# Second layer norm of an encoder block: scale and offset shared by VectorE, ScalarE and GpSimd, with gain and bias in PSUM

## The chip, the cores and the metric

The kernel runs on one core of one Trainium2 chip. The metric is device time in microseconds for one execution of the whole program; the median of three runs of the kernel before is 1250.47 us (1249.44 to 1252.44). Engines are named as in the profile: PE is TensorE, DVE is VectorE, ACT is ScalarE, POOL is GpSimd, and SP is SyncE, which issues most transfers. A name with a q (SPq, POOLq) is that engine's sequencer.

## The reference

One block of a bidirectional encoder over 1024 tokens of width 1024: a token mixer (projection, pooling, banded attention, gates), a layer norm, a mixture of 32 experts with two experts per token, and a second layer norm. The change is in the last line only.

```python
def layer_norm(x, g, b):
    xf = x.astype(jnp.float32)
    mu = jnp.mean(xf, axis=-1, keepdims=True)
    var = jnp.mean(jnp.square(xf - mu), axis=-1, keepdims=True)
    return ((xf - mu) * lax.rsqrt(var + LN_EPS) * g.astype(jnp.float32)
            + b.astype(jnp.float32)).astype(x.dtype)
...
        x = layer_norm(ALPHA * x + mix, ln1_g[l], ln1_b[l])
        ffn = hier_moe(x, w_router_group[l], b_router_group[l], w_router_expert[l],
                       b_router_expert[l], w_gate[l], w_up[l], w_down[l])
        x = layer_norm(ALPHA * x + ffn, ln2_g[l], ln2_b[l])
```

Here everything is float32, and `ln2_g`, `ln2_b` are vectors of 1024 numbers that lie along the free dimension of a tile, so they can't be given to an engine as one number per partition; mean and reciprocal root can.

## The kernel before

Tokens are cut into NT = 8 tiles of 128, one token per partition. Up to about 1209 us the program runs the mixer, the first layer norm and the expert blocks, with TensorE nearly always busy. The expert blocks add their outputs into the buffer `accd` in device memory, which already holds ALPHA times the first norm's result. A loop of zero or more rounds follows for tokens over an expert's capacity (`tc.For_i`, L1469; none here), with a barrier of all engines behind it. Then comes the second layer norm, the only part that the change touches, from L1491 to L1561.

In it SP loads the eight tiles `R[0]` to `R[7]` of 512 KB from `accd` (L1497); in the trace their tile is `r`. `MV[i0]` (`mv` in the trace) holds six columns for each tile of a pair: 0 the mean, 1 the variance, 2 the reciprocal root, 3 the square root, 4 a scaled mean of ACT's statistics, 5 minus half of the variance plus epsilon. `ln_gb2` (`ln_gb` in the trace) holds gain `ln_g2` and bias `ln_b2`, each copied to all partitions, in SBUF.

Statistics of a tile come from DVE (`stats_dve`, two BATCH_NORM_STATS2 and one AGGREGATE; tiles 0 and 2) or from ACT (`stats_act`, two passes with accumulation; tiles 1 and 3 to 7). `root` on ACT takes the square root, and `rstd2` on DVE makes the reciprocal root with one Newton step, for two tiles at a time: RECIPROCAL, two TENSOR_TENSOR, one SCALAR_TENSOR_TENSOR, each on 128x2 numbers. Then DVE alone passes twice over each tile: `scale` (L1536), (R - mean) * gain, and `finish2` (L1540), R * rstd + bias, behind which SP stores the tile (L1541). The last tile's second pass and store are cut in halves.

The order on each engine is the order in which the code is written (`tc.manual_schedule()`); each engine works its own list in order and waits by semaphores. Stores stand in SP's queue in the order written, too, and each waits there for its tile.

POOL has nothing to do in this part. Earlier it runs two-input elementwise work: L869 and L870 of the first layer norm (gain and bias, 128x1024), and L746, the low part of a split. The lines L826 and L827 (`rstd_of`) are DVE's own small steps there, on 128x1 numbers: both read two operands from SBUF. L92 is the helper `split`; where it reads `pT`, one operand lies in PSUM and the other in SBUF. L849 adds a PSUM tile to an SBUF tile.

Of the kernel before, what the change touches and what calls it, by code (L numbers as in the profile page):

```python
# [11 lines left out]
F32 = mybir.dt.float32  # L12
# [3 lines left out]
AF = mybir.ActivationFunctionType  # L16
ALU = mybir.AluOpType
AX = mybir.AxisListType
PSUM = bass.MemoryType.PSUM
# [3 lines left out]
D = 1024  # L23
NT = S // 128
# [9 lines left out]
EPS = 1e-5  # L34
# [15 lines left out]
def kernel(  # L50
# [8 lines left out]
    out = out[0]  # L59
# [7 lines left out]
    act, dve, pe, pool, sp = nc.scalar, nc.vector, nc.tensor, nc.gpsimd, nc.sync  # L67
# [6 lines left out]
    def bigtile(shape, dt, name):  # L74
        return big.tile(shape, dt, name=name, tag="b")
# [24 lines left out]
    HALF = [slice(0, 512), slice(512, 1024)]  # L100
# [383 lines left out]
    for b in range(NT + FILLS):  # L484
# [7 lines left out]
        if b >= NT:  # L492
            name = ("gate", "gate2")[b - NT]
# [904 lines left out]
    SPLIT, room, q = [], [], 0  # L1398
    for t, (b, p, c) in enumerate(SEQ):
        q = max(q, LOADS.index((p, c)))  # L1400
# [60 lines left out]
    ln_gb2 = bigtile([128, 2, D], F32, "ln_gb2")  # L1461
    ln_g2, ln_b2 = ln_gb2[:, 0], ln_gb2[:, 1]
    sp.dma_start(ln_g2, bcast(ln2_g, D))
    sp.dma_start(ln_b2, bcast(ln2_b, D))
    epst = const.tile([128, 1], F32, name="epst")
# [26 lines left out]
    R = {}  # L1492
    for i in range(0, NT, 2):
        t = bigtile([128, 2, D], F32, "r2")
# [2 lines left out]
            sp.dma_start(R[i + q], accd[(i + q) * 128:(i + q + 1) * 128])  # L1497


    MV = {}  # L1500
    for i0 in range(0, NT, 2):
        MV[i0] = lp2.tile([128, 2, 6], F32, name="mv2", bufs=NT // 2)

    def col(i, c):
        return MV[i - i % 2][:, i % 2, c:c + 1]

    def stats_act(i):

        junk = lp2.tile([128, D], F32, name="junk", bufs=1)
        act.activation(junk, R[i], AF.Copy, scale=-1.0 / (32 * D), accum_out=col(i, 4))  # L1510
        act.activation(col(i, 0), col(i, 4), AF.Copy, scale=-32.0)
        act.activation(junk, R[i], AF.Square, scale=1.0 / 32, bias=col(i, 4), accum_out=col(i, 1))  # L1512

    def stats_dve(i):
        st = lp2.tile([128, 2, 6], F32, name="bnst2")
        for c in range(2):
            dve.bn_stats(st[:, c, :], R[i][:, HALF[c]])
        dve.bn_aggr(MV[i - i % 2][:, i % 2, 0:2], st)

    def root(i0):  # L1520

        mv = MV[i0]
        act.activation(mv[:, :, 3], mv[:, :, 1], AF.Sqrt, bias=epst)  # L1523
        act.activation(mv[:, :, 5], mv[:, :, 1], AF.Copy, scale=-0.5, bias=-0.5 * EPS)

    def rstd2(i0):

        mv = MV[i0]
        r, t, u = mv[:, :, 2], mv[:, :, 3], mv[:, :, 5]
        dve.reciprocal(r, t)  # L1530
        dve.tensor_mul(t, r, r)  # L1531
        dve.tensor_mul(t, t, u)  # L1532
        dve.scalar_tensor_tensor(r, t, 1.5, r, op0=ALU.add, op1=ALU.mult)  # L1533

    def scale(i):
        dve.scalar_tensor_tensor(R[i], R[i], col(i, 0), ln_g2, op0=ALU.subtract, op1=ALU.mult)  # L1536

    def finish2(i):
        for sl in HALF if i == NT - 1 else [slice(0, D)]:
            dve.scalar_tensor_tensor(R[i][:, sl], R[i][:, sl], col(i, 2), ln_b2[:, sl], op0=ALU.mult, op1=ALU.add)  # L1540
            sp.dma_start(out[i * 128:(i + 1) * 128, sl], R[i][:, sl])  # L1541

    act.activation(lp2.tile([128, 1], F32, name="rt"), epst, AF.Sqrt)
    stats_dve(0)
    stats_act(1)
    root(0)
    stats_dve(2)
    stats_act(3)
    root(2)
    scale(0)  # L1550
    for i in range(4, NT):
        stats_act(i)
        if i % 2:
            root(i - 1)
    for i0 in range(0, NT, 2):
        if i0:
            scale(i0)
        scale(i0 + 1)
        rstd2(i0)
        finish2(i0)  # L1560
        finish2(i0 + 1)  # L1561


# [73 lines left out]
```

## Time and profile before

| | |
|---|---|
| median of 3 runs | 1250.47 us |
| the profiled execution's own time | 1252.02 us |
| its span in the profile | 1250.2 us |
| PE busy | 1157.9 us (93% of the span) |
| DVE busy | 907.7 us (73%) |
| ACT busy | 751.0 us (60%) |
| POOL busy | 264.8 us (21%) |
| the last expert block's matmuls end | about 1208.7 us |
| first load of the second layer norm is issued | 1214.75 us |
| last pass of DVE ends | 1246.0 us |

Times inside the profile are microseconds from the start of the span. The profiled execution took 1.8 us more than its span, and 1.55 us more than the median of the runs. The chain of waits is followed back from the last instruction; the timeline lists instructions in order of time with their duration, and "x2" stands for two of the same kind that follow each other; the windows view gives the busy time of each engine in a stretch. An instruction's duration in the timeline includes time that it spends waiting for something other than a semaphore.

### The profile page before, as it was taken

The page shows a single profiled execution, that of the slowest core. Times are in us where ns is not written, and L with a number is a line of the kernel's source. Part 1 is how long each engine was busy: PE and PEld are TensorE (multiplying, and loading weights), DVE is VectorE, ACT ScalarE, POOL GpSimd, SP SyncE. Part 2 cuts the span into 40 slices and gives each one's busy share as a digit, 9 for nine tenths or more (in the row PEclk, how much of TensorE's full clock was granted, in tenths as well). Part 3 has the DMA queues.
Part 4 walks back from the last instruction along what each step waited for, and adds up shares of the span by engine and source line. Part 5 has one row for each costly group of instructions (what it writes and reads, how often), then busy time and mean ns, then how long its engine had stood idle before and what let it go on. Part 6 is the DMA issues. An engine that isn't in the chain of part 4 may idle for free. (4 is left out here: it accounts for less than half of the span.)

```text
span 1250.2 us, 16049 instructions
## 1 busy us (share of the span) xinstructions
PE 1157.9 (93%) x5645; PEld 878.4 (70%) x5645; DVE 907.7 (73%) x1282; ACT 751.0 (60%) x989; POOL 264.8 (21%) x216
## 2 busy tenths in 40 slices
PE   8999999999999998999589999999999989989960
PEld 8888878888888886888468767766766656655630
DVE  4788972221853326899879999999978989988857
ACT  5577772111231114454458888888877887888745
POOL 2322200000000002466312222231222221232010
PEclk9999999999999998999689999999999999999995
DMA  8000104111121125635788999999999999999956
GB/s 272 1 1 1 45 17 122 51 51 42 35 76 40 37 102 183 263 135 217 240 320 327 366 390 396 364 375 374 351 330 357 348 391 376 365 385 395 400 159 236
DMA packets 91631, 279.36 MB, mean 223 GB/s; under 512 B 18989, under 2 KB 50733, under 8 KB 67869
## 3 DMA queue, kind: packets, MB, share of 16 engines
q1 hardware_dynamic: 83261, 252.15, 53.6%
q0 software_dynamic: 8288, 26.17, 8.4%
q8 instruction: 45, 0.74, 0.2%
q14 instruction: 37, 0.30, 0.1%
HBM read 252.32 MB, written 25.97 MB: 223 GB/s over the span
## 5 line engine op out<-in xcount | busy, mean ns | idle before, releaser
L1058 DVE TENSOR_TENSOR wel<-we,weh 128x2048 fp32r<-128x2048 f32 (+1 forms) x193 | 427.3, 2244 | 58.3 <-ACT weh L1056 56.6
L1056 ACT ACTIVATE weh<-we 128x2048 fp32r<-128x2048 f32 (+1 forms) x193 | 356.8, 1877 | 30.3 <-PE up L97 6.7
L1365 POOL DMA_INDIRECT accd<-y,psl x29 | 70.8, 2442 | 364.9 <-ACT y L1364 326.0
L646 ACT ACTIVATE sig<-gps,bch 128x512 f32<-128x512 f32 x29 | 19.9, 687 | 169.0 <-PE gps L98 169.0
L98 PE MATMUL gps<-xh,ghl 128*128 128x512 f32 x296 | 115.3, 390 | 0.0
L96 PE MATMUL gps<-xh,ghl 128*128 128x512 f32 x296 | 115.2, 389 | 0.0
L97 PE MATMUL gps<-xl,ghl 128*128 128x512 f32 x296 | 115.1, 389 | 0.0
L92 DVE TENSOR_TENSOR ghl<-wraw,ghl 128x1024 fp32r<-128x1024 f32 (+1 forms) x26 | 26.4, 1020 | 82.5 <-ACT ghl L91 82.5
L97 PE MATMUL gate<-wel,xinT 128*128 128x512 f32 (+7 forms) x176 | 70.8, 402 | 4.5 <-DVE wel L1058 4.5
L96 PE MATMUL yp<-weh,hT 128*128 128x512 f32 (+7 forms) x176 | 73.1, 415 | 0.1
L96 PE MATMUL gate<-weh,xinT 128*128 128x512 f32 (+7 forms) x176 | 70.7, 402 | 0.1
L98 PE MATMUL gate<-weh,xinT 128*128 128x512 f32 (+7 forms) x176 | 69.9, 397 | 0.0
L98 PE MATMUL yp<-weh,hT 128*128 128x512 f32 (+7 forms) x176 | 69.8, 397 | 0.0
L97 PE MATMUL yp<-wel,hT 128*128 128x512 f32 (+7 forms) x176 | 69.6, 395 | 0.0
L96 PE MATMUL up<-weh,xinT 128*128 128x512 f32 (+7 forms) x176 | 69.5, 395 | 0.0
L97 PE MATMUL up<-wel,xinT 128*128 128x512 f32 (+7 forms) x176 | 68.9, 391 | 0.0
L98 PE MATMUL up<-weh,xinT 128*128 128x512 f32 (+7 forms) x176 | 68.9, 391 | 0.0
L96 PEld LDWEIGHTS gps<-xh,ghl 128*128 128x128 f32 x296 | 55.6, 188 | 11.7
L97 PEld LDWEIGHTS gps<-xl,ghl 128*128 128x128 f32 x296 | 55.6, 188 | 11.6
L98 PEld LDWEIGHTS gps<-xh,ghl 128*128 128x128 f32 x296 | 55.6, 188 | 11.6
L1268 POOL DMA_INDIRECT xin<-x1d,psl x29 | 55.1, 1900 | 12.1 <-issue 5.2
L96 PE MATMUL z<-woh,mhl 128*128 128x512 f32 x128 | 52.7, 412 | 4.3 <-DVE sig L668 4.3
(342 smaller groups left out, 2690.4 us busy)
## 6 DMA issues: line engine op xcount, KB each, us to landing
we<-in_w_gate_dram SPq DMA_DIRECT2D x62, 1024.0 KB
we<-in_w_up_dram SPq DMA_DIRECT2D x62, 1024.0 KB
we<-in_w_down_dram SPq DMA_DIRECT2D x60, 1024.0 KB
wraw<-in_w_in_dram SPq DMA_DIRECT2D x20, 512.0 KB
x<-in_x_dram SPq DMA_DIRECT2D x8, 512.0 KB
wo<-in_w_o_dram SPq DMA_DIRECT2D x4, 1024.0 KB
xr<-in_x_dram SPq DMA_DIRECT2D x8, 512.0 KB
x1d<-x1p SPq DMA_DIRECT2D x8, 512.0 KB
```

The costliest lines, as they stand in the source:

```text
L92: dve.tensor_sub(lo, src, f(hi))
L96: pe.matmul(ps, lh, rh, start=first, stop=False)
L97: pe.matmul(ps, lh, rl, start=False, stop=False)
L98: pe.matmul(ps, ll, rh, start=False, stop=last)
L646: act.activation(dst[:, HALF[half]], ps, fn, bias=bch[:, bcol:bcol + 1])
L1056: act.activation(hi[:, sl], raw, AF.Copy)
L1058: dve.tensor_sub(lo[:, sl], raw, f(hi[:, sl]))
L1268: pool.indirect_dma_start(out=XIN[b][:n], out_offset=None, in_=x1d, in_offset=bass.IndirectOffsetOnAxis(ap=slot0 if b == 0 else IDX[b][:n, ...
L1365: pool.indirect_dma_start(out=accd, out_offset=bass.IndirectOffsetOnAxis(ap=IDX[b][:n, 0:1], axis=0), in_=y[:n], in_offset=None, compute_o ...
```

## The change

The gain and the bias are first copied by ACT into a PSUM tile `gbp` (four pieces of 128x512). The passes over the tiles are then divided:

- Tile 0: POOL alone, a TENSOR_SCALAR (subtract the mean, multiply by rstd) and two TENSOR_TENSOR (gain, bias).
- Tile 1: ACT does the normalisation (`Identity` with scale and bias; DVE makes the bias -mean * rstd, L1577), POOL gain and bias.
- Tiles 2, 3, 4: DVE does `scale` with the gain from PSUM in two halves, ACT multiplies by rstd (`times`), POOL adds the bias.
- Tiles 5, 6, 7: DVE does `scale` and `offset`, both in halves with the second operand from PSUM.

The statistics of tiles 4 and 6 go from ACT to DVE. `root` and `rstd2` run for tile 0 and tile 1 apart. SP's stores stand in the order 0, 1, 5, 2, 6, 3, 7 (two halves); tile 4 is stored from ACT's queue at its end.

```diff
--- before.py
+++ after.py
@@ -1497,6 +1497,13 @@
             sp.dma_start(R[i + q], accd[(i + q) * 128:(i + q + 1) * 128])
 
 
+    lpp = ctx.enter_context(tc.tile_pool(name="lpp", bufs=1, space=PSUM, reuse_waits="tile"))
+    gbp = lpp.tile([128, 2, D], F32, name="gbp")
+    for c in range(2):
+        for half in range(2):
+            act.activation(gbp[:, c, HALF[half]], ln_gb2[:, c, HALF[half]], AF.Copy)
+
+
     MV = {}
     for i0 in range(0, NT, 2):
         MV[i0] = lp2.tile([128, 2, 6], F32, name="mv2", bufs=NT // 2)
@@ -1517,48 +1524,88 @@
             dve.bn_stats(st[:, c, :], R[i][:, HALF[c]])
         dve.bn_aggr(MV[i - i % 2][:, i % 2, 0:2], st)
 
-    def root(i0):
-
-        mv = MV[i0]
-        act.activation(mv[:, :, 3], mv[:, :, 1], AF.Sqrt, bias=epst)
-        act.activation(mv[:, :, 5], mv[:, :, 1], AF.Copy, scale=-0.5, bias=-0.5 * EPS)
-
-    def rstd2(i0):
-
-        mv = MV[i0]
-        r, t, u = mv[:, :, 2], mv[:, :, 3], mv[:, :, 5]
+    def root(*ii):
+
+        mv, q = MV[ii[0] - ii[0] % 2], slice(ii[0] % 2, ii[-1] % 2 + 1)
+        act.activation(mv[:, q, 3], mv[:, q, 1], AF.Sqrt, bias=epst)
+        act.activation(mv[:, q, 5], mv[:, q, 1], AF.Copy, scale=-0.5, bias=-0.5 * EPS)
+
+    def rstd2(*ii):
+
+        mv, q = MV[ii[0] - ii[0] % 2], slice(ii[0] % 2, ii[-1] % 2 + 1)
+        r, t, u = mv[:, q, 2], mv[:, q, 3], mv[:, q, 5]
         dve.reciprocal(r, t)
         dve.tensor_mul(t, r, r)
         dve.tensor_mul(t, t, u)
         dve.scalar_tensor_tensor(r, t, 1.5, r, op0=ALU.add, op1=ALU.mult)
 
+    def store2(i, sl=slice(0, D), eng=sp):
+        eng.dma_start(out[i * 128:(i + 1) * 128, sl], R[i][:, sl])
+
     def scale(i):
-        dve.scalar_tensor_tensor(R[i], R[i], col(i, 0), ln_g2, op0=ALU.subtract, op1=ALU.mult)
-
-    def finish2(i):
-        for sl in HALF if i == NT - 1 else [slice(0, D)]:
-            dve.scalar_tensor_tensor(R[i][:, sl], R[i][:, sl], col(i, 2), ln_b2[:, sl], op0=ALU.mult, op1=ALU.add)
-            sp.dma_start(out[i * 128:(i + 1) * 128, sl], R[i][:, sl])
+        for sl in HALF:
+            dve.scalar_tensor_tensor(R[i][:, sl], R[i][:, sl], col(i, 0), gbp[:, 0, sl], op0=ALU.subtract, op1=ALU.mult)
+
+    def offset(i):
+        for sl in HALF:
+            dve.scalar_tensor_tensor(R[i][:, sl], R[i][:, sl], col(i, 2), gbp[:, 1, sl], op0=ALU.mult, op1=ALU.add)
+            if i == NT - 1:
+                store2(i, sl)
+        if i < NT - 1:
+            store2(i)
+
+    def times(i):
+        act.activation(R[i], R[i], AF.Copy, scale=col(i, 2))
 
     act.activation(lp2.tile([128, 1], F32, name="rt"), epst, AF.Sqrt)
     stats_dve(0)
+    root(0)
+    rstd2(0)
     stats_act(1)
-    root(0)
     stats_dve(2)
+    root(1)
+    rstd2(1)
+
+    pool.tensor_scalar(R[0], R[0], col(0, 0), col(0, 2), op0=ALU.subtract, op1=ALU.mult)
+    pool.tensor_mul(R[0], R[0], ln_g2)
+    pool.tensor_add(R[0], R[0], ln_b2)
+    store2(0)
+    scale(2)
     stats_act(3)
-    root(2)
-    scale(0)
-    for i in range(4, NT):
-        stats_act(i)
-        if i % 2:
-            root(i - 1)
-    for i0 in range(0, NT, 2):
-        if i0:
-            scale(i0)
-        scale(i0 + 1)
-        rstd2(i0)
-        finish2(i0)
-        finish2(i0 + 1)
+    mv = MV[0]
+
+    dve.scalar_tensor_tensor(mv[:, 1, 4:5], mv[:, 1, 0:1], -1.0, mv[:, 1, 2:3], op0=ALU.mult, op1=ALU.mult)
+    act.activation(R[1], R[1], AF.Identity, scale=col(1, 2), bias=col(1, 4))
+    pool.tensor_mul(R[1], R[1], ln_g2)
+    pool.tensor_add(R[1], R[1], ln_b2)
+    store2(1)
+    root(2, 3)
+    stats_dve(4)
+    scale(3)
+    rstd2(2, 3)
+    stats_act(5)
+
+    for i in (2, 3):
+        times(i)
+        pool.tensor_add(R[i], R[i], ln_b2)
+    root(4, 5)
+    scale(4)
+    stats_dve(6)
+    rstd2(4, 5)
+    times(4)
+    pool.tensor_add(R[4], R[4], ln_b2)
+    stats_act(7)
+    root(6, 7)
+    scale(5)
+    offset(5)
+    store2(2)
+    scale(6)
+    scale(7)
+    rstd2(6, 7)
+    offset(6)
+    store2(3)
+    offset(7)
+    store2(4, eng=act)
 
 
 # ---- launch: one core; inputs and outputs as the reference has them ----
```

How the instructions then stand on three engines. In these rows `r_10751` holds tiles 0 and 1, `r_10754` tiles 2 and 3, `r_10757` tiles 4 and 5, `r_10760` tiles 6 and 7; `mv_10771` to `mv_10774` are the columns of the same pairs after the change, and a line number is that of the version it stands in.

DVE, in the kernel before, from the first tile's scale to the first offset of the second pair:

```order
-L1536 SCALAR_TENSOR_TENSOR r_10751<-r_10751,mv_10763,ln_gb_10549 128x1024 x2
-L1530 RECIPROCAL mv_10763<-mv_10763 128x2
-L1531 TENSOR_TENSOR mv_10763<-mv_10763 128x2
-L1532 TENSOR_TENSOR mv_10763<-mv_10763 128x2
-L1533 SCALAR_TENSOR_TENSOR mv_10763<-mv_10763 128x2
-L1540 SCALAR_TENSOR_TENSOR r_10751<-r_10751,mv_10763,ln_gb_10549 128x1024 x2
-L1536 SCALAR_TENSOR_TENSOR r_10754<-r_10754,mv_10764,ln_gb_10549 128x1024 x2
```

The same engine in the changed kernel, from `rstd2(1)` to `rstd2(2, 3)`:

```order
+L1537 RECIPROCAL mv_10771<-mv_10771 128x1
+L1538 TENSOR_TENSOR mv_10771<-mv_10771 128x1
+L1539 TENSOR_TENSOR mv_10771<-mv_10771 128x1
+L1540 SCALAR_TENSOR_TENSOR mv_10771<-mv_10771 128x1
+L1547 SCALAR_TENSOR_TENSOR r_10754<-r_10754,mv_10772,gbp 128x512 x2
+L1577 SCALAR_TENSOR_TENSOR mv_10771<-mv_10771 128x1
+L1524 BN_STATS bnst_10818<-r_10757 128x6 x2
+L1525 BN_AGGR mv_10773<-bnst_10818 128x2
+L1547 SCALAR_TENSOR_TENSOR r_10754<-r_10754,mv_10772,gbp 128x512 x2
+L1537 RECIPROCAL mv_10772<-mv_10772 128x2
+L1538 TENSOR_TENSOR mv_10772<-mv_10772 128x2
+L1539 TENSOR_TENSOR mv_10772<-mv_10772 128x2
```

The passes over tiles 0 and 1 have left DVE, the passes read `gbp`, and the small steps of `rstd2` stand between them as before.

POOL, behind the loop's barrier:

```order
-L1632 UNCONDITIONAL_BRANCH
-L1632 ISA
+L1569 ISA
+L1569 TENSOR_SCALAR r_10751<-r_10751,mv_10771 128x1024
+L1570 TENSOR_TENSOR r_10751<-r_10751,ln_gb_10549 128x1024
+L1571 TENSOR_TENSOR r_10751<-r_10751,ln_gb_10549 128x1024
+L1579 TENSOR_TENSOR r_10751<-r_10751,ln_gb_10549 128x1024
+L1580 TENSOR_TENSOR r_10751<-r_10751,ln_gb_10549 128x1024
+L1590 TENSOR_TENSOR r_10754<-r_10754,ln_gb_10549 128x1024 x2
+L1596 TENSOR_TENSOR r_10757<-r_10757,ln_gb_10549 128x1024
+L1679 UNCONDITIONAL_BRANCH
+L1679 ISA
```

POOL had only its end here; now it has one TENSOR_SCALAR and seven TENSOR_TENSOR on SBUF, ahead of which the program selects the engine's code library again (the ISA row of L1569).

SP's stores:

```order
-L1541 DMA out_dram<-r_10751 128x1024 x2
-L1541 DMA out_dram<-r_10754 128x1024 x2
-L1541 DMA out_dram<-r_10757 128x1024 x2
-L1541 DMA out_dram<-r_10760 128x1024
-L1541 DMA out_dram<-r_10760 128x512 x2
-L1632 UNCONDITIONAL_BRANCH
+L1543 DMA out_dram<-r_10751 128x1024 x2
+L1543 DMA out_dram<-r_10757 128x1024
+L1543 DMA out_dram<-r_10754 128x1024
+L1543 DMA out_dram<-r_10760 128x1024
+L1543 DMA out_dram<-r_10754 128x1024
+L1543 DMA out_dram<-r_10760 128x512 x2
```

Tile 5 now goes ahead of tile 2, and tile 6 ahead of tile 3, in a queue that works in order; the store of tile 4 has left it.

## Rows read from the trace of the kernel before

**Rows 1.** Windows view: stretch, its us, then busy us (instructions) of PE, PEld, DVE, ACT, POOL, clock, DMA share, GB/s
```profile
1215.00:1218.50 3.50, 0.00 (x0) 0.00 (x0) 0.00 (x0) 1.49 (x2) 0.00 (x0) 0.50 0.79 249
1218.50:1246.00 27.50, 0.00 (x0) 0.00 (x0) 24.84 (x39) 16.25 (x38) 0.00 (x0) 0.50 0.62 243
```

**Rows 2.** Chain of waits, near its end: start us, us, what
```profile
1242.73 0.17 DVE mv L1531
...
1245.34 0.66 DVE r L1540
```

**Rows 3.** Timeline of the second layer norm: start us, us, engine, line, what
```profile
1214.75 3.94 SPq L1497 DMA_DIRECT2D r<-accd  x8
...
1218.55 1.29 DVE L1517 BATCH_NORM_STATS2 bnst<-r 128x6 f32<-128x512 f32 x2 [9.06 <-DMA r<-accd]
1219.82 1.06 ACT L1510 ACTIVATE junk<-r 128x1024 f32<-128x1024 f32 x1 [3.14 <-DMA r<-accd]
...
1221.79 1.29 DVE L1517 BATCH_NORM_STATS2 bnst<-r 128x6 f32<-128x512 f32 x2 [1.71 <-DMA r<-accd]
...
1222.37 0.30 ACT L1523 ACTIVATE mv<-mv,epst 128x2 f32<-128x2 f32 x1
...
1226.44 2.48 DVE L1540 SCALAR_TENSOR_TENSOR r<-r,mv,ln_gb 128x1024 f32<-128x1024 f32 x2
...
1227.76 18.61 SPq L1541 DMA_DIRECT2D out_dram<-r  x9
...
1243.40 2.61 DVE L1540 SCALAR_TENSOR_TENSOR r<-r,mv,ln_gb 128x1024 f32<-128x1024 f32 x3
```

**Rows 4.** Timeline of POOL, in the first layer norm, 529 to 538 us
```profile
529.98 2.38 POOL L869 TENSOR_TENSOR x1p<-x1p,ln_gb 128x1024 f32<-128x1024 f32 x1 [2.61 <-ACT x1p L864]
532.44 2.40 POOL L870 TENSOR_TENSOR x1p<-x1p,ln_gb 128x1024 f32<-128x1024 f32 x1
534.80 2.38 POOL L746 TENSOR_TENSOR mhl<-mg,mhl 128x1024 fp32r<-128x1024 f32 x1
```

**Rows 5.** Timeline of DVE in the same stretch
```profile
529.93 1.28 DVE L852 BATCH_NORM_STATS2 bnst<-xr 128x6 f32<-128x512 f32 x2
...
532.42 0.16 DVE L827 SCALAR_TENSOR_TENSOR mv<-mv 128x1 f32<-128x1 f32 x1
532.61 2.24 DVE L826 SCALAR_TENSOR_TENSOR mv<-mv 128x1 f32<-128x1 f32 x1
534.89 2.31 DVE L827 SCALAR_TENSOR_TENSOR mv<-mv 128x1 f32<-128x1 f32 x1
537.23 0.22 DVE L826 SCALAR_TENSOR_TENSOR mv<-mv 128x1 f32<-128x1 f32 x1
```

**Rows 6.** Timeline of POOL and DVE, in the attention, 84 to 88 us
```profile
84.20 1.43 POOL L172 TENSOR_TENSOR qtmp<-q,rope 128x256 f32<-128x256 f32 x2 [11.56 <-DVE q L245]
...
84.87 1.27 DVE L92 TENSOR_TENSOR pl<-pT,ph 128x512 fp32r<-128x512 f32 x2
```

**Rows 7.** Groups of instructions, shapes apart: operation, count, then busy us, mean ns, idle before
```profile
L849 DVE SCALAR_TENSOR_TENSOR xr<-xr,z 128x512 f32<-128x512 f32 x16 | 10.3, 681 | 0.3 <-PE z L98 0.3
...
L1056 ACT ACTIVATE weh<-we 128x1024 fp32r<-128x1024 f32 x8 | 7.9, 1052 | 0.0
...
L711 POOL MEMSET zt<- 128x1024 f32 x1 | 0.9, 946 | 0.0
L702 POOL CAST tri<-trif 128x256 bf16<-128x256 f32 x1 | 0.7, 737 | 39.0 <-DMA trif<-in_c_tri_dram 39.0
```

**Rows 8.** One line, L1632, the program's end: ns min/median/max, first and last start
```profile
L1632 SPq EVENT_SEMAPHORE  x7: 17/28/28, 1249.0 to 1250.2; - x7
...
L1632 POOLq DRAIN  x3: 46/98/7176, 1215.0 to 1250.0; - x3
```

**Rows 9.** Windows view again, stretches of the stores' transfers
```profile
1227.80:1228.80 1.00, 0.00 (x0) 0.00 (x0) 1.00 (x1) 0.97 (x3) 0.00 (x0) 0.50 0.24 94
1228.80:1229.20 0.40, 0.00 (x0) 0.00 (x0) 0.40 (x2) 0.40 (x1) 0.00 (x0) 0.50 1.01 410
...
1248.00:1248.80 0.80, 0.00 (x0) 0.00 (x0) 0.00 (x0) 0.00 (x0) 0.00 (x0) 0.50 0.33 123
```

## Prediction, written before the result was known

> **What bounds the kernel now.** I read the windows first. Between 1218.5 and 1246.0 us DVE is busy for 24.84 of 27.5 us, ACT for 16.25 and POOL for none [rows 1]; before that DVE waits for the first load. The chain of waits agrees: from the loads on it runs through DVE, down to the last half pass at 1245.34 [rows 2]. So in this stage DVE's list sets the end, with the stores behind it. From the timeline I take DVE's prices: statistics of a tile 1.5 (two of 1.29 together, and an aggregate), a full pass 1.2 to 1.25 (two take 2.48), a half pass 0.66 [rows 2, 3], and the four small steps of `rstd2` 0.75 (four of 0.17 with gaps) [rows 2].
>
> The other limit is behind the last pass. A store issued at 1227.76 has data moving for 0.24 of the window that ends at 1228.8, so it starts some 0.8 us after its issue and then runs at about 400 GB/s, 1.31 us for 512 KB [rows 3, 9]. The last data end near 1248.27 (0.33 of the window from 1248.0), SP sees that at 1249.0, and 1.2 us later the span ends [rows 8, 9]: 1.95 us after the last data.
>
> **The change, part by part.**
>
> *Copies to PSUM.* Four ACT copies of 128x512, about half of 1.05 us each plus a wait, 2.7 us in all [rows 7]. They start at 1215.2, where ACT's table load starts today, and with that load end at 1219.4. The first statistics end only at 1220.1 [rows 3], so the loads hide them: cost 0.
>
> *Passes.* DVE had sixteen full passes; it keeps nine, each in two halves from PSUM. A half with a PSUM operand took 0.68 alone (L849) [rows 7], in pairs 1.2 to 1.4 with the ends taken from these rows; I take 1.3. It gains two tiles of statistics (2 x 1.5) and 0.9 us for one more `rstd2` and L1577. Net: 16 x 1.22 = 19.5 becomes 9 x 1.3 + 3.9 = 15.6. That alone would be worth about 4 us of DVE's time.
>
> *POOL.* Seven TENSOR_TENSOR of 128x1024 at 2.38 to 2.40 us, 0.08 apart where one waits for the other [rows 4]. The TENSOR_SCALAR has no row. Below, the one-operand MEMSET of the same size, 0.95; above, the CAST's 0.74 for 256 columns, which a rate like TENSOR_TENSOR's carries to 2.4 [rows 7]. I take 1.7, between them. POOL's first work could start at 1221.2, when `rstd2(0)` is done. But POOL's drain at the end of the program, begun at 1215.0, lasts 7.18 us [rows 8]: something holds the engine until 1222.2. I take 1222.2 and keep 1221.2 as the lower end.
>
> *What POOL does to DVE.* This decides. In the first layer norm DVE runs steps on 128x1 numbers beside POOL's 2.4 us instructions. Unhindered they take 0.16 to 0.22; beside POOL two take 2.24 and 2.31, and each ends within 0.05 us of the end of the POOL instruction beside it (532.44 + 2.40 = 534.84; 532.61 + 2.24 = 534.85) [rows 4, 5]. In the gap between two POOL instructions of which one waits for the other, two DVE steps slip through; between independent ones, one. The steps held read two operands from SBUF. BATCH_NORM_STATS2 with one is not held: 1.28 under L869, as in the last stage [rows 3 to 5]. TENSOR_TENSOR with one operand in PSUM is not held either: 1.27 for two under L172 [rows 6]. So the passes from PSUM are free, but `rstd2` isn't: three of its four steps read two SBUF operands, and DVE's list is in order, so all passes behind wait too.
>
> *The sum*, us from the span's start (ACT: statistics 2.5, root 0.3, a copy 1.1 [rows 3, 7]):
> - POOL, tile 0: 1222.2 + 1.7, then gain and bias, ends 1228.8.
> - `rstd2(1)` is asked for at 1223.4 (ACT's statistics of tile 1 end at 1223.0) and is through only at 1228.85; unhindered 1224.2.
> - DVE: scale 2 and L1577 to 1230.35. ACT to 1231.5. POOL, tile 1: 1231.5 to 1236.4.
> - DVE: statistics 4, scale 3, reciprocal at 1233.3; `rstd2(2, 3)` is held until 1236.45.
> - ACT's product for tile 2 at 1237.55; POOL's biases 2 and 3 to 1242.4. DVE: scale 4, statistics 6, at 1239.4; `rstd2(4, 5)` is held until 1242.65.
> - ACT: product 4, statistics 7, root, 1246.5. DVE: scale 5, offset 5, scale 6, scale 7 (4 x 1.3) to 1247.85; POOL's last bias ends at 1246.2, so `rstd2(6, 7)` runs free to 1248.6; offsets 6 and 7 to 1249.9 and 1251.2.
>
> DVE ends 5.2 us later than the 1246.0 of today: the three holds cost 9.9 us (4.65, 3.15 and 3.25, the last two less the 0.55 that three steps take anyway), more than what is saved. *Stores:* store 3 stands behind store 6 in SP's queue, so stores 6, 3 and both halves of 7 come together: from 1249.95 + 0.8, 1.5 MB take 3.94, data end 1254.7, span end 1256.6. That is 6.4 us over 1250.2. The profiled execution's own time would go from 1252.0 to 1258.4; it lies 1.55 over the median, so against the median I say **1256.9 us**.
>
> Its own bounds: POOL from 1221.2 with 0.95 for TENSOR_SCALAR takes off 1.75, with 2.4 adds 0.7; the seven pairs of half passes on this path at 1.2 or 1.4 move it by 0.7 either way. So 1254.5 to 1258.3.
>
> **Rivals.**
>
> *N, no holding worth its name.* If 128x1 and 128x2 steps slip past POOL, `rstd2` costs 0.75 each time. Then ACT's order sets the pace (product 3 at 1232.1, `rstd2(4, 5)` at 1233.1), DVE ends at 1241.7, POOL at 1241.2, stores 6, 3, 4 and 7 come together from 1241.25 (5.25 us of data), and the span ends at 1248.45: 1.8 less, 1248.7 us. It decides from the point where the three holdings together fall below about 4.5 us. For it: one or two steps do slip through at each gap. Against: the rows show 2.3 us for a single 128x1 step, and POOL's list leaves only 0.08 us gaps. 12%, on either side of -0.2%.
>
> *P, the per-partition number counts as an SBUF operand.* Each half pass reads the tile and a column of `mv`, and no row has this form beside POOL; L849's factor is a constant. Then scale 3's halves get one POOL gap each, scale 4's second half and the first of offset 5 wait out one bias each: about 3.5 us more, 1260.4. Against: L92 under L172. 8%.
>
> *L, POOL starts late.* The drain of 7.18 us says that POOL can be occupied unseen [rows 8]; if its first work waits about 6 us longer, to 1228.2, `rstd2(1)` escapes (1224.2), but `rstd2(2, 3)`, asked for at 1228.5, is through at 1232.4, `rstd2(4, 5)` at 1239.75, and `rstd2(6, 7)` waits for the last bias, 1246.9. Offset 6 ends at 1248.6, the span at 1255.4: 1255.6 us, 1.3 less than my sum, since a hold is traded for a hold. 6%.
>
> The Trainium skill gives such a delay a cause: GPSIMD Engine Reference, Instruction dispatch, says that the first call into freshly loaded code pays about 6 us with no instruction shown. By that rule the time would be that of rival L; the drain neither proves nor excludes it. On holding, SBUF - State Buffer, Who interferes with whom, says that a GpSimd instruction that reads SBUF and a VectorE one with two SBUF inputs exclude each other for the whole instruction, and that a VectorE instruction with at most one doesn't contend. By this rule N is out, and the trace agrees with 2.24 and 2.31 us; it speaks against this change, whose `rstd2` keeps such steps.
>
> **How the numbers follow.** The forecast with its bounds has 70%, L 6%, P 8%, N 12%, and 4% is for what I haven't seen. The range 1253.0 to 1261.0 takes in the forecast, L and P, with 1.5 us below for holds that are shorter than I think; it leaves out N. A measurement here can tell some 0.2%, 2.5 us, from no change. Faster by more needs N with cheaper stores: 6%. Within 0.2%: N as computed, and part of the rest, 10%. Slower: 84%.
>
> **What would show it.** In the profile after, single steps of L1538 to L1540 of 2 us and more that end with a POOL instruction, some 10 us in all; half passes of 0.6 to 0.7 us under POOL; POOL's first instruction near 1222; the end of DVE near 1251; and full DMA from there to 1254.7. Steps of 0.2 us throughout would refute me, half passes of 2 us would be P, and a first POOL instruction at 1227 or later would be L.

## The result, and the profile after

The changed kernel takes **1257.31 us** in the median of four runs (1256.67 to 1259.38); the kernel before took 1250.59 in four (1249.44 to 1252.44). The ratio is 1.0056, with an interval of 1.0041 to 1.0070: slower by 5.1 to 8.8 us. The profiled execution of the changed kernel took 1257.18 us with a span of 1255.4.

The stage is best compared from the issue of its first load to the end of the span, since the part ahead of it varies by a microsecond or two: 1214.75 to 1250.23 before, 35.48 us; 1214.47 to 1255.40 now, 40.93. That is 5.45 us more.

Windows view of the changed kernel, the first row over the same stretch as the second of [rows 1], the other two over the last stores' transfers, behind DVE's end at 1249.82 (columns as there):

```profile
1218.50:1246.00 27.50, 0.00 (x0) 0.00 (x0) 25.77 (x43) 16.21 (x36) 20.14 (x8) 0.50 0.44 176
...
1250.30:1253.20 2.90, 0.00 (x0) 0.00 (x0) 0.00 (x0) 0.00 (x0) 0.00 (x0) 0.50 1.01 391
1253.20:1254.00 0.80, 0.00 (x0) 0.00 (x0) 0.00 (x0) 0.00 (x0) 0.00 (x0) 0.50 0.19 69
```

POOL has taken over 20.14 us of work, and yet DVE shows more busy time than before, 25.77 against 24.84. The timeline tells why. DVE and POOL of the changed kernel, in the order of time (ACT and SP left out):

```profile
1221.34 3.79 POOL L1569 TENSOR_SCALAR r<-r,mv 128x1024 f32<-128x1024 f32 x1 [9.84 <-DVE mv L1540]
...
1223.44 0.16 DVE L1538 TENSOR_TENSOR mv<-mv 128x1 f32<-128x1 f32 x1
1223.70 0.16 DVE L1539 TENSOR_TENSOR mv<-mv 128x1 f32<-128x1 f32 x1
...
1225.22 2.34 POOL L1570 TENSOR_TENSOR r<-r,ln_gb 128x1024 f32<-128x1024 f32 x1
1225.29 2.29 DVE L1577 SCALAR_TENSOR_TENSOR mv<-mv 128x1 f32<-128x1 f32 x1
...
1229.96 2.34 POOL L1579 TENSOR_TENSOR r<-r,ln_gb 128x1024 f32<-128x1024 f32 x1
...
1230.41 1.92 DVE L1538 TENSOR_TENSOR mv<-mv 128x2 f32<-128x2 f32 x1
...
1232.38 2.34 POOL L1580 TENSOR_TENSOR r<-r,ln_gb 128x1024 f32<-128x1024 f32 x1
1232.43 2.31 DVE L1539 TENSOR_TENSOR mv<-mv 128x2 f32<-128x2 f32 x1
...
1236.20 4.64 POOL L1590 TENSOR_TENSOR r<-r,ln_gb 128x1024 f32<-128x1024 f32 x2 [1.48 <-ACT r L1558]
...
1237.75 0.81 DVE L1538 TENSOR_TENSOR mv<-mv 128x2 f32<-128x2 f32 x1
1238.67 2.19 DVE L1539 TENSOR_TENSOR mv<-mv 128x2 f32<-128x2 f32 x1
...
1242.29 1.40 DVE L1551 SCALAR_TENSOR_TENSOR r<-r,mv,gbp 128x512 f32<-128x512 f32 x2
1242.32 2.37 POOL L1596 TENSOR_TENSOR r<-r,ln_gb 128x1024 f32<-128x1024 f32 x1 [1.48 <-ACT r L1558]
...
1247.10 2.72 DVE L1551 SCALAR_TENSOR_TENSOR r<-r,mv,gbp 128x512 f32<-128x512 f32 x4
```

Five steps on one or two numbers per partition, 0.16 us each when free, take 2.29, 1.92, 2.31, 0.81 and 2.19: 9.5 us, of which 8.7 is waiting. Each begins under a TENSOR_TENSOR of POOL and ends with it, to 0.02 or 0.03 us (1225.22 + 2.34 = 1227.56; 1225.29 + 2.29 = 1227.58), like the rows of the first layer norm in [rows 4, 5]. The TENSOR_SCALAR at the top holds nobody at 1223.44, and the half passes at 1242.29, which start 0.03 us before a TENSOR_TENSOR, run at their free price.

The chain of waits names the same steps, where it had L1531 with 0.17 before [rows 2]. Chain of the changed kernel from the loads on, its longest pieces:

```profile
1214.47 4.03 DMA r<-accd
1225.37 2.20 DVE mv L1577
1230.41 1.93 DVE mv L1538
1232.43 2.32 DVE mv L1539
1238.67 2.20 DVE mv L1539
```

The two ends, as in [rows 8]; view of the program's last line, which is L1679 now:

```profile
L1679 SPq EVENT_SEMAPHORE  x7: 17/28/28, 1253.8 to 1255.3; - x7
L1679 POOLq DRAIN  x3: 50/104/9602, 1242.3 to 1255.1; - x3
```

SP sees the last store at 1253.8, against 1249.0 before. So the 5.2 us by which the span is longer are: 3.8 at DVE's end (1249.82 against 1246.01), 1.0 because three stores of 512 KB now come together behind it (4.0 us from DVE's end to SP's sight, 3.0 before), 0.4 in the last steps behind that (1.57 against 1.19).

### The profile page after: what moved, and what is told of

It is laid out like the page before. It is cut to its first block, busy times and chain, and to the rows that moved or that the text cites. A ratio compares the mean times of both kernels' runs of the same rounds, so it can differ in the third digit from the quotient of the medians.

```text
span 1255.4 us, 16066 instructions
## 1 busy us (share of the span) xinstructions
PE 1157.8 (92%) x5645; PEld 878.0 (70%) x5645; DVE 912.7 (73%) x1294; ACT 753.5 (60%) x989; POOL 284.4 (23%) x224
## 4 chain that ended last, share of the span: by engine, by line
PE 67%; DMA 11%; DVE 11%; ACT 5%; issue 4%; POOL 1%; SPq 0%; DVEq 0%; POOLq 0%; ACTq 0%
PE gps L98 5%; PE gps L96 5%; PE gps L97 5%; DVE wel L1058 4%; DMA we<-in_w_up_dram 3%; DMA we<-in_w_down_dram 3%; ACT weh L1056 3%; PE yp L96 3%; DMA we<-in_w_gate_dram 3%; PE gate L97 2%; PE yp L97 2%; PE yp L98 2%; PE gate L98 2%; PE gate L96 2%; PE yps L97 2%
## 5 line engine op out<-in xcount | busy, mean ns | idle before, releaser
L1056 ACT ACTIVATE weh<-we 128x2048 fp32r<-128x2048 f32 (+1 forms) x193 | 357.2, 1877 | 33.6 <-DMA we<-in_w_down_dram 7.7
```

Source lines behind the costliest of these rows:

```text
L1056: act.activation(hi[:, sl], raw, AF.Copy)
```

## The experiments

Kernel before, beside these runs: 1250.80 us in the first four, 1250.95 in the last four. Intervals are those of the ratio to it. The first, third and fourth ask what holds DVE and what the new instructions cost, the others what sets the end of the program. The intervals of the change, of the other store order and of the passes from SBUF overlap, and so do those of the one-operand steps alone, with the other store order and with tile 4 on DVE. Differences between these rest on the traces as well, on the stage from the first load's issue to the end of the span.

### The small steps with one operand

```diff
-        dve.tensor_mul(t, r, r)
-        dve.tensor_mul(t, t, u)
-        dve.scalar_tensor_tensor(r, t, 1.5, r, op0=ALU.add, op1=ALU.mult)
+        for i in ii:
+            dve.tensor_scalar(col(i, 3), col(i, 2), col(i, 2), col(i, 5), op0=ALU.mult, op1=ALU.mult)
+        for i in ii:
+            dve.tensor_scalar(col(i, 2), col(i, 3), 1.5, col(i, 2), op0=ALU.add, op1=ALU.mult)
...
-    dve.scalar_tensor_tensor(mv[:, 1, 4:5], mv[:, 1, 0:1], -1.0, mv[:, 1, 2:3], op0=ALU.mult, op1=ALU.mult)
+    dve.tensor_scalar(mv[:, 1, 4:5], mv[:, 1, 0:1], -1.0, mv[:, 1, 2:3], op0=ALU.mult, op1=ALU.mult)
```

The same arithmetic, with the second factor given as a number per partition.

> The three steps of rstd2 and L1577 become TENSOR_SCALAR on one column, with the second factor given as a column per partition, so that each reads one tile operand from SBUF; nothing else changes. Holding theory: five steps were held for 2.29, 1.92, 2.31, 0.81 and 2.19 us beside GpSimd; all fall to about 0.2 us, VectorE ends near 1242 instead of 1249.8, and the time falls from 1257.3 by 5 to 7 us, to 1250.3 to 1252.5 (the lower value if the stores set the end, the upper if GpSimd's drain of 7.2 us behind its last bias does). Rival A, GpSimd's own chain of 20 us is what VectorE waits for through ScalarE: the steps are short but idle time takes their place, 1257 within 1 us. Rival B, the column per partition counts as an operand: the steps stay at 2 us, 1257 or more.

Measured: 1251.05 us, ratio 1.0000 (0.9991 to 1.0009), against 1.0056 for the change itself. The timeline of DVE and POOL shows the steps free under POOL:

```profile
1225.31 2.35 POOL L1571 TENSOR_TENSOR r<-r,ln_gb 128x1024 f32<-128x1024 f32 x1
1225.37 0.21 DVE L1578 TENSOR_SCALAR mv<-mv 128x1 f32<-128x1 f32 x1
...
1227.74 2.35 POOL L1572 TENSOR_TENSOR r<-r,ln_gb 128x1024 f32<-128x1024 f32 x1
1228.21 0.16 DVE L1537 RECIPROCAL mv<-mv 128x2 f32<-128x2 f32 x1
1228.48 0.45 DVE L1539 TENSOR_SCALAR mv<-mv 128x1 f32<-128x1 f32 x2
1228.85 0.33 DVE L1541 TENSOR_SCALAR mv<-mv 128x1 f32<-128x1 f32 x2
```

DVE ends 27.25 us after the first load is issued, against 35.35 in the change and 31.25 before. So the holding by POOL costs DVE 8.1 us, and without it the change would give DVE 4.0. A column given as a number per partition doesn't count as an operand that is held. But the 4.0 us bring nothing, and that was new: DVE and POOL are both through at 1241.8, SP sees the last store at 1247.0, and the span ends at 1249.8. In the change the span ended 1.6 us behind SP's sight of the last store; here that would be 1248.6. The view of the last line shows what is late:

```profile
L1680 SPq EVENT_SEMAPHORE  x7: 17/28/28, 1247.0 to 1249.8; - x7
L1680 POOLq DRAIN  x3: 50/104/14968, 1234.0 to 1249.5; - x3
```

POOL's drain, recorded from 1234.01 on while POOL still has additions to do, ends at 1248.98. That is 7.2 us behind POOL's last addition (1241.78). In the change it ends 7.2 us behind it, too: 1242.28 + 9.60 = 1251.88, against 1244.68. Before, it took 7.18 us from 1215.0 [rows 8], when POOL had been through since 1211.8. So the drain itself takes 7.2 us from when POOL is through and the drain issued, and here the program ends 0.8 us behind it. What the drain does in that time no run shows.

### The stores in another order

```diff
     scale(5)
+    store2(2)
+    store2(3)
     offset(5)
-    store2(2)
...
     offset(6)
-    store2(3)
     offset(7)
```

> Only SyncE's queue order changes: stores 2 and 3 stand ahead of store 5, where their tiles are ready, so that behind the last passes only stores 6 and 7 are left. Holding theory with the stores as second limit: VectorE is unchanged (ends near 1249.8), the last data end about 1.3 us earlier (512 KB at 400 GB/s), 1256.0 against 1257.3. Rival: the transfers hide behind the last pass anyway or GpSimd's drain sets the end, no change within 0.4 us.

Measured: 1255.93 us, ratio 1.0041 (1.0027 to 1.0055), 1.4 less than the change. The holds are the same (2.21, 2.32 and 2.20 in the chain of waits); SP sees the last store 2.7 us behind DVE's end (1248.78 to 1251.48) instead of 4.0. The stage is 39.3 us instead of 40.9. That is the share of the stores that had piled up behind tile 6.

### The passes from SBUF

```diff
-            dve.scalar_tensor_tensor(R[i][:, sl], R[i][:, sl], col(i, 0), gbp[:, 0, sl], op0=ALU.subtract, op1=ALU.mult)
+            dve.scalar_tensor_tensor(R[i][:, sl], R[i][:, sl], col(i, 0), ln_g2[:, sl], op0=ALU.subtract, op1=ALU.mult)
...
-            dve.scalar_tensor_tensor(R[i][:, sl], R[i][:, sl], col(i, 2), gbp[:, 1, sl], op0=ALU.mult, op1=ALU.add)
+            dve.scalar_tensor_tensor(R[i][:, sl], R[i][:, sl], col(i, 2), ln_b2[:, sl], op0=ALU.mult, op1=ALU.add)
```

> VectorE's scale and offset take gain and bias from SBUF instead of PSUM, still in halves; the copies to PSUM stay and go unused. Holding theory (any VectorE instruction with two tile operands in SBUF waits for a GpSimd instruction that runs beside it): the halves of scale 3 and of offset 5 are held up to 2.4 us each, part of it in place of holds of the small steps, 2 to 4 us slower than the change, 1259 to 1261. Rival: only the tiny steps are held, through something in their start; the half passes stay at 0.65 to 0.75 us and the time at 1257 or 0.3 less.

Measured: 1259.61 us, ratio 1.0071 (1.0057 to 1.0085), 2.3 more than the change. The timeline of DVE and POOL:

```profile
1227.86 4.36 DVE L1547 SCALAR_TENSOR_TENSOR r<-r,mv,ln_gb 128x512 f32<-128x512 f32 x2
1228.88 2.79 POOL L1579 TENSOR_TENSOR r<-r,ln_gb 128x1024 f32<-128x1024 f32 x1
...
1242.27 3.50 DVE L1551 SCALAR_TENSOR_TENSOR r<-r,mv,ln_gb 128x512 f32<-128x512 f32 x2
1242.29 2.93 POOL L1596 TENSOR_TENSOR r<-r,ln_gb 128x1024 f32<-128x1024 f32 x1 [1.48 <-ACT r L1558]
```

Two half passes take 4.36 and 3.50 us where they took 1.36 and 1.40 from PSUM. POOL pays as well: 2.79 and 2.93 instead of 2.34 and 2.37. The instruction is the same in both kernels and only the place of one operand differs, so PSUM as the second operand is what keeps the passes free under a TENSOR_TENSOR.

Beside the TENSOR_SCALAR the passes from SBUF are free, too, two halves in 1.41 us. Same run and view:

```profile
1220.26 3.80 POOL L1569 TENSOR_SCALAR r<-r,mv 128x1024 f32<-128x1024 f32 x1 [9.33 <-DMA r<-accd]
...
1222.89 1.41 DVE L1547 SCALAR_TENSOR_TENSOR r<-r,mv,ln_gb 128x512 f32<-128x512 f32 x2
```

### TENSOR_SCALAR in place of the bias

```diff
-        pool.tensor_add(R[i], R[i], ln_b2)
+        pool.tensor_scalar(R[i], R[i], col(i, 0), col(i, 2), op0=ALU.subtract, op1=ALU.mult)
...
-    pool.tensor_add(R[4], R[4], ln_b2)
+    pool.tensor_scalar(R[4], R[4], col(4, 0), col(4, 2), op0=ALU.subtract, op1=ALU.mult)
```

> GpSimd's bias additions for tiles 2, 3 and 4 are replaced by TENSOR_SCALAR of the form of L1569, so the bias of these tiles is left out and they are scaled once too often. Theory C: the 3.79 us of L1569 hold a first-call cost, later ones take about 1.1 us. Theory D: 3.79 us is the steady price. Either way, if TENSOR_SCALAR on GpSimd does not hold VectorE, as beside L1569, the steps of rstd2 for tiles 4 and 5 are not held (0.81 and 2.19 us before), and VectorE ends about 3 us earlier than 1249.8; if it holds, they wait as before.

Measured: 1257.04 us (one run). The kernel leaves out the bias of tiles 2 to 4, and only its times are read. The timeline of DVE and POOL, from the third bias on:

```profile
1235.87 7.54 POOL L1590 TENSOR_SCALAR r<-r,mv 128x1024 f32<-128x1024 f32 x2 [1.50 <-ACT r L1558]
...
1237.40 0.17 DVE L1538 TENSOR_TENSOR mv<-mv 128x2 f32<-128x2 f32 x1
1237.67 0.16 DVE L1539 TENSOR_TENSOR mv<-mv 128x2 f32<-128x2 f32 x1
...
1243.39 3.78 POOL L1596 TENSOR_SCALAR r<-r,mv 128x1024 f32<-128x1024 f32 x1
1243.40 0.17 DVE L1538 TENSOR_TENSOR mv<-mv 128x2 f32<-128x2 f32 x1
1243.68 0.91 DVE L1539 TENSOR_TENSOR mv<-mv 128x2 f32<-128x2 f32 x1
1244.62 0.16 DVE L1540 SCALAR_TENSOR_TENSOR mv<-mv 128x2 f32<-128x2 f32 x1
```

3.8 us is its steady price, not that of a first call. It lets two-operand steps of DVE pass, except for one that came 0.3 us after its start and was kept until 1.2 us after it. DVE ends 33.69 us after the first load's issue, 1.7 earlier than in the change (about 3 had been expected), and the total hardly moves, since POOL now ends at 1247.17 and its drain at 1254.37, 0.8 us ahead of the span's end at 1255.2.

### One-operand steps and the other order of stores

The first two edits together (the diffs above).

> The one-operand steps of e1_one_operand together with the store order of e2_store_order. Drain theory: in e1_one_operand GpSimd's last bias ends at 1241.8, its drain 7.2 us later at 1249.0, and only then the program ends (1249.8), while the stores were seen complete at 1247.5; so earlier stores bring nothing, 1251.0 as e1_one_operand within 0.5. Rival, the stores set the end as in the change: 1.3 us less, 1249.7.

Measured: 1250.50 us, ratio 0.9998 (0.9989 to 1.0008): no gain over the one-operand steps alone. It does not test what earlier stores would bring, since they don't come earlier: this execution began the stage 1.6 us sooner, and from the first load's issue SP sees the last store after 33.0 us, against 32.6 with the one-operand steps alone. Tile 5, stored 21.1 us after the first load there, waits here behind tile 3 until 25.5. What it does show is that stores 0.4 us later don't matter: POOL is through after 27.35 us in both kernels, the drain ends at 1247.37, 7.2 us behind POOL, and the span at 1248.2, a stage of 35.4 us in both. The last line:

```profile
L1680 SPq EVENT_SEMAPHORE  x7: 17/28/28, 1245.8 to 1248.2; - x7
L1680 POOLq DRAIN  x3: 50/104/14963, 1232.4 to 1247.9; - x3
```

### The kernel before, with one late GpSimd step

```diff
         finish2(i0 + 1)
+    pool.tensor_mul(lp2.tile([128, 1], F32, name="late"), R[NT - 1][:, D - 1:], R[NT - 1][:, D - 1:])
```

> The kernel before, with one useless GpSimd TENSOR_TENSOR on 128x1 numbers behind the last pass over tile 7; it writes to a tile that nobody reads. Drain theory: GpSimd's drain takes 7.2 us behind its last work whenever that is, so it ends at 1246.1 + 7.2 = 1253.3 and the span at 1254.2, 4.0 us later than before, 1254.8. Rival: the drain of 7.18 us in the kernel before was what was left of earlier indirect transfers; 1250.8 within 0.5.

Measured: 1255.06 us, ratio 1.0031 (1.0020 to 1.0043), 4.1 us for one useless instruction of 0.19. Timeline of POOL, and the last line's view:

```profile
1247.05 0.19 POOL L1562 TENSOR_TENSOR late<-r 128x1 f32<-128x1 f32 x1 [34.99 <-DVE r L1540]
```

```profile
L1633 SPq EVENT_SEMAPHORE  x7: 17/28/28, 1250.0 to 1255.2; - x7
L1633 POOLq DRAIN  x3: 46/104/7437, 1247.0 to 1255.0; - x3
```

SP sees the last store at 1250.0; the span ends at 1255.27, 0.8 us behind the drain (1247.01 + 7.44 = 1254.45). So late work on POOL by itself moves the end.

### Tile 4 finished on DVE

```diff
-    times(4)
-    pool.tensor_add(R[4], R[4], ln_b2)
     stats_act(7)
     root(6, 7)
+    offset(4)
...
-    store2(4, eng=act)
```

On top of the one-operand steps; tile 4 is stored from SP's queue.

> e1_one_operand with tile 4's offset on VectorE (two half passes, 1.35 us) in place of ScalarE's product and GpSimd's last bias; its store is in SyncE's queue behind tile 5's. Drain theory: GpSimd ends 2.4 us earlier (1239.4), the drain at 1246.6; VectorE ends at 1243.0 and the stores then set the end, 1248.4: 1.4 us under e1_one_operand, 1249.6. Rival, VectorE's list sets the end of e1_one_operand: 1.3 us more, 1252.4.

Measured: 1249.68 us, ratio 0.9991 (0.9982 to 0.9999). POOL ends at 1238.32 and its drain at 1245.52; now the stores are last (SP sees the last one at 1245.86, and the span ends 1.6 us later, at 1247.4, as in the change).

### Less work on POOL, and stores in the order of readiness

```diff
+    def shared(i):
+        act.activation(R[i], R[i], AF.Identity, scale=col(i, 2), bias=col(i, 4))
+        pool.tensor_mul(R[i], R[i], ln_g2)
+        pool.tensor_add(R[i], R[i], ln_b2)
+        store2(i)
...
+    shared(0)
     rstd2(1)
-
-    pool.tensor_scalar(R[0], R[0], col(0, 0), col(0, 2), op0=ALU.subtract, op1=ALU.mult)
...
+    offset(4)
     scale(5)
+    store2(2)
     offset(5)
-    store2(2)
     scale(6)
+    store2(3)
```

One-operand steps, tile 4 finished on DVE, the normalisation of tile 0 on ACT instead of POOL's TENSOR_SCALAR, and stores in the order in which tiles come ready. ACT's roots for tiles 4 and 5 also stand ahead of its products for tiles 2 and 3.

> One-operand steps; tile 0 is normalised by ScalarE (Identity, like tile 1) in place of GpSimd's TENSOR_SCALAR of 3.8 us; tile 4's offset goes from ScalarE and GpSimd to VectorE; stores in the order 0, 1, 4, 2, 5, 3, 6, 7. Holding and drain theory: GpSimd has six TENSOR_TENSOR from 1224.6 to 1239.0, its drain ends at 1246.2; VectorE ends at 1242.9 and the last store is complete near 1246; span 1247.1 to 1247.4, that is about 1248, 2.5 to 3 us faster than before. If ScalarE's added pass delays the statistics instead, VectorE waits and the time stays near 1250.

Measured: **1247.11 us**, ratio 0.9966 (0.9953 to 0.9979), 3.8 us under the kernel before beside it, where 2.5 to 3 had been expected, and 10 under the change. Windows view, columns as before:

```profile
1218.50:1246.00 27.50, 0.00 (x0) 0.00 (x0) 22.30 (x55) 15.90 (x35) 14.01 (x6) 0.50 0.67 266
```

and the last line:

```profile
L1678 SPq EVENT_SEMAPHORE  x7: 17/28/28, 1244.9 to 1246.4; - x7
L1678 POOLq DRAIN  x3: 46/104/12539, 1232.7 to 1246.2; - x3
```

SP's sight of the last store (1244.9) and the end of the drain (1232.68 + 12.54 = 1245.22) lie 0.3 us apart. The stores still set the end: the span ends at 1246.5, 1.6 us behind SP's sight. DVE ends later than with the one-operand steps alone (28.07 us after the first load's issue against 27.25), and yet the program is shorter: POOL is through 3.5 us earlier on the same count (23.9 against 27.3).

The stage, from the issue of the first load to the end of the span, puts the kernels in nearly the order of the medians (us):

| kernel | DVE through, from the first load's issue | stage | median |
|---|---|---|---|
| before | 31.25 | 35.5 | 1250.59 |
| the change | 35.35 | 40.9 | 1257.31 |
| one-operand steps | 27.25 | 35.4 | 1251.05 |
| other store order | 35.05 | 39.3 | 1255.93 |
| passes from SBUF | 38.09 | 43.7 | 1259.61 |
| TENSOR_SCALAR for the bias | 33.69 | 41.4 | 1257.04 (one run) |
| one-operand steps, other store order | 27.27 | 35.4 | 1250.50 |
| late GpSimd step | 31.94 | 40.3 | 1255.06 |
| tile 4 on DVE | 28.08 | 33.6 | 1249.68 |
| balanced | 28.07 | 32.3 | 1247.11 |

## Why the prediction came out

**Direction and mechanism: right.** The text gave 1256.9 us, by the holding of the small steps under POOL. The one-operand steps take that holding away, with the same arithmetic on the same engine, and the loss goes. The text's two sums for DVE hold as well: "worth about 4 us of DVE's time" against 4.0 (31.25 to 27.25), and holds of 9.9 us against 8.7.

**The rule on two-operand steps** (the Trainium skill, SBUF - State Buffer, Who interferes with whom) agrees with the TENSOR_TENSORs of POOL in this stage: steps held for up to 2.31 us, 4.36 for two half passes from SBUF. It doesn't agree with the TENSOR_SCALAR, which reads SBUF as well: steps of 0.16 us beside one of 3.79, and two half passes from SBUF in 1.41 beside one of 3.80. There the measurement decides.

**What failed in the steps.** The term on TENSOR_SCALAR was mis-sized: 1.7 was taken between bounds of 0.95 and 2.4 [rows 7], and it takes 3.79, beyond the upper one. Its rows were a MEMSET and a cast, neither of which does two operations with numbers per partition. The hold that was to come from it didn't: `rstd2(1)` was forecast through at 1228.85 and is at 1224.06. In its place L1577, which the text let run free, was held for 2.29 us. So the first hold cost 2.1 us instead of 4.65, `rstd2(2, 3)` is through at 1234.94 instead of 1236.45, and DVE ends at 1249.82, not 1251.2. The span came to 1255.4, not 1256.6.

A smaller reading fails, too: that two steps slip through the gap between POOL instructions of which one waits for the other. In the stretch of [rows 5], only L827 passes at 532.42; the L826 ahead of it (532.05, 0.33 us) had itself been held up to the gap. At the gap of 0.08 us at 1232.3 none passed.

The closeness of the total, 0.4 us, is in part luck. In the profiled pair the change costs 5.2 us of span, not the 6.4 of the sum; between the medians it is 6.7. The profiled execution of before lay 1.4 us over its median, that of the change 0.1 under, so the 1.55 us that the text took off for the median more than made up for a span that it had 1.2 us too long.

**The drain: misread.** "Something holds the engine until 1222.2" is wrong. POOL began at 1221.34, near the lower end of the text's bounds (1221.2); the 7.18 us [rows 8] are the price of the drain itself. It cost the forecast little here, since the drain ends at 1251.9, ahead of the stores. But it priced rival N wrongly. The one-operand steps are N made real, and DVE and POOL ended as N said, at 1241.7 and 1241.8 against 1241.7 and 1241.2. Yet the span ended at 1249.8 instead of 1248.45, and the gain N promised is not there.

**The other rivals.** N, no holding, is refuted by five held steps. P, that a column as a number per partition counts as an operand, is refuted by twelve half passes of L1547, 0.70 to 0.74 us each, and six of L1551, 0.74 to 0.75, under POOL or not. L, a late start of POOL, is refuted by 1221.34, 0.1 us after its input was ready. The delay of about 6 us that the Trainium skill (GPSIMD Engine Reference, Instruction dispatch) gives to a first call doesn't show: the first call took 3.79, later ones 3.77 and 3.78. Whether code was loaded in POOL's idle time ahead of it (9.84 us), no run shows.

**Smaller terms.** TENSOR_TENSOR of POOL 2.34 to 2.37 for 2.38 to 2.40; two half passes 1.36 to 1.40 alone and four in a row 2.72, for 1.3 a pair; the copies to PSUM cost nothing, DVE's first statistics starting at 1218.53 against 1218.55. The stores piled up as forecast: 3.94 us of data were expected, and transfers are at full share from 1250.3 to 1253.2. The other store order gave 1.4 us of that back, between the medians.

**Still open.** Why a TENSOR_SCALAR with two columns takes 1.6 times as long as a TENSOR_TENSOR, and why it holds DVE only near its start: one step showed that, and no run takes it apart. Nor does any run show what the drain does in its 7.2 us.

## What to carry to other kernels

Before work is moved to GpSimd, list the instructions of VectorE that will run beside it and read two SBUF operands: a step of 0.16 us on a single column is held for a whole 2.3 us instruction, and all that is queued behind it waits. Written with one tile and a number per partition, or with one operand in PSUM, the same arithmetic was not held here. A TENSOR_SCALAR on GpSimd let such steps pass here, but took 3.8 us. And let GpSimd finish well before the last store is seen, since the end of the program waits for its drain: 5.2 us before was too late here (one-operand steps), 6.9 was enough (the last experiment).

## What the runs showed of the hardware that was not expected

- POOL's drain at the program's end takes 7.2 us from when POOL is idle and the drain issued, whatever ran last: 7.18 before, 7.20 in the change, 7.2 behind a step of 0.19 us and behind TENSOR_SCALARs. Hidden before and in the change, it set the end in four of the eight experiments (one-operand steps alone and with the other store order, TENSOR_SCALAR for the bias, the late step).
- A TENSOR_SCALAR of 128x1024 on POOL takes 3.8 us each time, and two-operand steps and half passes of DVE ran at their free price beside it, but for one step of 0.91 us that began 0.3 us after its start.
- The holding is mutual: three TENSOR_TENSORs of POOL that began while a half pass from SBUF was under way took 2.67 to 2.93 us instead of 2.34 to 2.37.
